# Two-layer hybrid trunk: the last norm's sums on ScalarE, residual steps behind each head's output on GpSimd, and a new order of TensorE's work in the tail

## The chip, the cores and the metric

The kernel runs on one core of a Trainium2 chip, as one launch. The metric is the device time of the launch in microseconds, the median of a few runs. The engines are TensorE (PE; its weight loads are listed apart as PEld), VectorE (DVE), ScalarE (ACT), GpSimd (POOL) and SyncE (SP), which only issues DMAs here. Each engine takes its own instructions strictly in order; between engines they wait on semaphores.

## The reference

Five blocks of 128 tokens (`TT = 5`: four latent blocks, and one context block with the index `TS = 4`), width 1024, two layers, float32. Layer 0 is gated attention. Layer 1 is a gated linear recurrence with 8 heads of 128, run in both directions. Cut to what this change touches:

```python
for i in range(DEPTH):                      # DEPTH = 2
    sh, sc, g = _adaln(cond, ada_w[i], ada_b[i])
    h = x * (1.0 + sc) + sh
    if i % 2 == 0:
        out, ... = attention(h, ...)
    else:
        out, s_fw, s_bw = _rec_mix(h, s0_fw, s0_bw, w_in, lb, norm_gain, w_out)
    x = _layer_norm(DEEPNORM_ALPHA * x + g * out, ln_gain[i], ln_bias[i])

def _rec_mix(...):                          # per head
    q, f_fw, f_bw, i_in, g = split(h @ w_in)
    o = scan forward (k_fw, v, log f_fw) + scan backward (k_bw, v, log f_bw)
    o = _rms_norm(o, norm_gain)
    return (o * silu(g)) @ w_out, s_fw, s_bw

def _layer_norm(x, g, b):
    mu  = mean(x);  var = mean((x - mu) ** 2)
    return (x - mu) * rsqrt(var + LN_EPS) * g + b
```

## The kernel before

Products of float32 matrices are made as three matmuls of split operands: a rounded part (`hi`, a cast on ScalarE, line 223) and the rest (`lo`, a subtraction on VectorE, line 224). `split_piece` makes both from a weight piece that SyncE has loaded.

**Layer 1, the loop over heads.** `proj_gen(h)` makes head h's projections: long runs of matmuls into `vgps` and `rps`, evacuated to `A` (keys and queries of both directions), `T` (decays), `v` and `g`. `gla_gen(h)` is the recurrence, in steps that end in a `yield`: seven *levels* (`lev` 0 to 6, blocks of 1 to 64 tokens: 20 small matmuls into `lv`, then on VectorE the keys, line 1276, the decays, line 1280, and the queries, line 1281, scaled for the next level; up to level 3 a copy `kc` on ScalarE; after level 4 a further block `dg`, and four copies into `At` on GpSimd, line 1295), then the *key turn* (`kp`, transposes), the *states* (`sp`), the output (`op`: squares on ScalarE, `rsqrt` into `rstdo`, two VectorE instructions, lines 1343 and 1345), and the last turn (`oT`, then `ghi` on ScalarE and `glo` on VectorE). The steps of head h are laid between the projections of head h + 1 by the class `Lane`, which counts the TensorE time that the main generator yields and compares it with due times (`D_GLA`, `D_LEV`, `D_KT`, `D_ST`, `D_OUT`). So TensorE has projection matmuls between two levels. A scheduler then orders each engine's instructions by what is ready and by where the code emitted them; what is pinned with `keep_in_program_order` stays as written.

`rsqrt` is a scale-and-add on VectorE (line 191, `rs_t`) and a power on GpSimd (line 192).

**Residual steps.** The class `Residual` prepares what the last norm adds: for each of 4 column pieces and 5 token blocks it loads 128x256 of layer 0's output (`rx<-x1d`), multiplies by `ln_g` (line 1379), adds `ln_b` (line 1380) and stores it (`x1a<-rx`), all on GpSimd's queue, all pinned. One `residual.step()` finishes the pieces that the step before loaded, and loads up to two more. `gla_gen` calls it twice a head: at the end of level 4, after the copies into `At`, and in the output step behind `rsqrt`. Thirteen steps do all 20 pieces.

**The tail.** After the last projections only head 7's recurrence is left. Now `weave` lays one step of `tail_gen` behind each step of that recurrence. A step has products of the output projection of layer 1 (`out_part(tt, ks)`: token block tt, heads ks, six matmuls of 512 columns for each head), splits of `w_out` (`wo_split(n)`), and *spreads*: `spread(1, i, ...)` makes a quarter of the gate rows `gate[1]`, 128 rows from a column by four matmuls with an identity (`gateps`, eight passes in the profile), and a copy of the bank to SBUF on VectorE (line 308). PSUM holds four tiles of two banks: token blocks 0 and 1 (later 2) keep one each, and everything else takes turns in the rest. Then `Norm(1, tt)` finishes the five blocks in order: blocks 0 to 2 lack head 7 alone, blocks 3 and 4 are whole. `part` multiplies by the gate (line 1026), adds the residual (line 1027) and takes `bn_stats` (line 1028); `finish` takes the aggregate (line 1033), `rsqrt`, and scales (lines 1042 and 1043, in two halves of 512 columns), and stores one half from SyncE and one from ScalarE. Block 4 comes in four parts of 256 columns.

Of the kernel before, what the change touches and what calls it, by code (L numbers as in the profile page):

```python
# [11 lines left out]
F32 = mybir.dt.float32  # L12
F32R = mybir.dt.float32r
U8 = mybir.dt.uint8
AF = mybir.ActivationFunctionType
ALU = mybir.AluOpType
AX = mybir.AxisListType

P = 128
D = 1024  # L20
KT = D // P
TS = 4
TT = 5
NT = TT * P
CW = 256
# [7 lines left out]
LN_EPS = 1e-5  # L33
# [99 lines left out]
def hybrid_step(ctx: ExitStack, tc: tile.TileContext, a: dict, o: dict):  # L133
    nc = tc.nc
# [53 lines left out]
    def rsqrt(out, in_, scale, eps):  # L188
        n = in_.shape[-1]
        t = tiny.tile([P, NKV * TT], F32, tag="rs", name="rs_t")  # L190
        nc.vector.tensor_scalar(t[:, :n], in_, scale, eps, ALU.mult, ALU.add)  # L191
        nc.gpsimd.tensor_tensor(out, t[:, :n], mhalf[:, :n], ALU.pow)
# [105 lines left out]
        nc.vector.tensor_tensor(gcol, src, bias, ALU.add)  # L298
        return None if layer else lambda: spread(layer, c4, gcol)

    def spread(layer, c4, gcol):

        ps = bank1("gateps")
        for s in range(2):
            for j in range(2):
                col = bass.AP(gcol.tensor, gcol.offset + 2 * j + s, [list(gcol.ap[0]), [0, P]])
                nc.tensor.matmul(ps[:, (2 * s + j) * P:(2 * s + j + 1) * P], col, ident, start=True, stop=True)
        nc.vector.tensor_copy(gate[layer][:, :, c4 * CW:(c4 + 1) * CW], ps[:].rearrange("p (a b) -> p a b", a=2))

    def ada_gen(chunks):  # L310
        todo, last = None, None
# [73 lines left out]
    gate = [None, None]  # L385
# [622 lines left out]
    class Norm:  # L1008
        def __init__(self, layer, tt, ps=None, parts=2):
            self.layer, self.tt, self.w = layer, tt, D // parts  # L1010
            if layer == 0:
                ps = bank2("outp")
            self.ps = ps and [ps[:, nh, :] for nh in range(2)]
            if layer == 0:
                self.x = lnp.tile([P, D], F32, tag="x", name="x", bufs=2)
                nc.scalar.dma_start(self.x, xd[tt])
            else:
                self.x = resid.pop(tt)
            self.y = lnp.tile([P, D], F32, tag="y", name="y", bufs=2)
            self.st = tiny.tile([P, parts, 6], F32, tag=f"st{parts}", name="st")  # L1020

        def part(self, n, ps):
            s = slice(n * self.w, (n + 1) * self.w)
            y = self.y[:, s]
            g = gate[self.layer][:, 1 if self.tt == TS else 0, s]
            nc.vector.tensor_tensor(y, ps, g, ALU.mult)  # L1026
            nc.vector.scalar_tensor_tensor(y, self.x[:, s], ALPHA, y, ALU.mult, ALU.add)  # L1027
            nc.vector.bn_stats(self.st[:, n, :], y)  # L1028

        def finish(self):  # L1030
            x, y = self.x, self.y
            mv = tiny.tile([P, 2], F32, tag="mv", name="mv")
            nc.vector.bn_aggr(mv, self.st[:].rearrange("p a b -> p (a b)"))  # L1033
            rt = tiny.tile([P, 8], F32, tag="rstd", name="rstdl")
            rstd = rt[:, 0:1]
            rsqrt(rstd, mv[:, 1:2], 1.0, LN_EPS)
            for nh in range(2):
                s = slice(nh * 512, (nh + 1) * 512)
                if self.layer == 0:
                    nc.vector.tensor_scalar(y[:, s], y[:, s], mv[:, 0:1], rstd, ALU.subtract, ALU.mult)  # L1040
                else:
                    nc.vector.scalar_tensor_tensor(x[:, s], y[:, s], mv[:, 0:1], lng[:, s], ALU.subtract, ALU.mult)  # L1042
                    nc.vector.scalar_tensor_tensor(x[:, s], x[:, s], rstd, lnb[:, s], ALU.mult, ALU.add)  # L1043
                    (nc.sync, nc.scalar)[nh].dma_start(yd[self.tt][:, s], x[:, s])
            if self.layer == 0:
                nc.sync.dma_start(x1d[self.tt], y)

    drain(split_gs(range(6, 8)))
    h1hi = gsp.tile([P, KT, NT], F32R, tag="gs", name="h1hi")
# [178 lines left out]
    def gla_gen(h, H, last=False):  # L1228
# [30 lines left out]
        for lev in range(7):  # L1259
            nb = NT // (2 * w)  # L1260
            pt = wide(bank2("lv"))
            for c in range(TT):
                if lev < 5:
                    for b in range(4):
                        t0 = c * P + 32 * b
                        queue(nc.tensor.matmul(pt[32 * b:32 * b + 32, 32 * c:32 * c + 32], kc[:, t0:t0 + 32],  # L1266
                                               view(A, QB + t0, [[2 * w, 16 // w], [QF - QB + w, 2], [1, w]]),
                                               start=True, stop=True), c + b == 0)
                else:
                    for b in range(P // w):  # L1270
                        ko, qo = (KB, QB) if b % 2 else (KF, QF)
                        s0, t0 = c * P + w * b, c * P + w * (b ^ 1)
                        queue(nc.tensor.matmul(pt[w * b:w * b + w, w * c:w * c + w], A[:, ko + s0:ko + s0 + w],
                                               A[:, qo + t0:qo + t0 + w], start=True, stop=True), c + b == 0)
            kv = view(A, KF, [[KB - KF + w, 2], [2 * w, nb], [1, w]])
            nc.vector.tensor_tensor(kv, kv, view(cur, 1, [[2 * nb - 1, 2], [2, nb], [0, w]]), ALU.mult)
            if lev < 4:
                kc = kcopy(2 * w)
            qv = view(A, QB, [[QF - QB + w, 2], [2 * w, nb], [1, w]])
            nc.vector.tensor_tensor(view(nxt, 0, [[1, 2 * nb]]), view(cur, 0, [[2, 2 * nb]]), view(cur, 1, [[2, 2 * nb]]), ALU.mult)  # L1280
            nc.vector.tensor_tensor(qv, qv, view(cur, 2 * nb + 1, [[-2 * nb - 1, 2], [2, nb], [0, w]]), ALU.mult)
            if lev == 0:
                nc.scalar.copy(near, pt[:, :32 * TT])
            elif lev < 5:
                merge(lev, pt)
            if lev == 4:
                pt = wide(bank2("dg"))
                for c in range(TT):
                    for b in range(4):
                        t = slice(c * P + b * 32, c * P + (b + 1) * 32)  # L1290
                        nc.tensor.matmul(pt[32 * b:32 * b + 32, 32 * c:32 * c + 32], H["kd"][:, t], H["q"][:, t], start=True, stop=True)
                merge(0, pt)
                for b in range(4):
                    r = slice(32 * b, 32 * b + 32)
                    nc.gpsimd.tensor_copy(blocks(At[r, :], P)[:, :, r], blocks(near[r, :], 32))  # L1295
                residual.step()
            elif lev > 4:
                for b in range(P // w):
                    r, o_ = slice(w * b, w * b + w), slice(w * (b ^ 1), w * (b ^ 1) + w)
                    nc.scalar.copy(blocks(At[r, :], P)[:, :, o_], blocks(pt[r, :w * TT], w))  # L1300
            cur, nxt = nxt, cur
            w *= 2
            yield D_LEV
# [35 lines left out]
            nc.scalar.activation(on[:, cc], opw[:, cc], AF.Square, accum_out=ss[:, c:c + 1])  # L1339
        rstd = tiny.tile([P, 8], F32, tag="rstd", name="rstdo")  # L1340
        rsqrt(rstd[:, :TT], ss[:, :TT], 1.0 / P, NORM_EPS)
        residual.step()
        nc.vector.tensor_tensor(on[:].rearrange("p (a b) -> p a b", a=TT), opw[:, :NT].rearrange("p (a b) -> p a b", a=TT),
                                view(rstd, 0, [[1, TT], [0, P]]), ALU.mult)
# [68 lines left out]
    def out_part(tt, ks):  # L1413
        if tt not in outs:
            outs[tt] = bank2("outp")
        for k in ks:
            for nh in range(2):
                out_mms(outs[tt][:, nh, :], tt, nh, ghi, glo, [k], queued=(k, nh) == (ks[0], 0))

    for h in range(RH):  # L1420
        H = {} if h else H
        for n, dt in enumerate(proj_gen(h, H, False) if h else first):
            lane.advance(dt)
            if h == RH - 1 and n in (12, 14, 20, 21):
                wo_split((12, 14, 20, 21).index(n))
        if h == RH - 1:
            out_part(0, (0, 1))
        lane.add(gla_gen(h, H, h == RH - 1))
    while residual.todo or residual.live:
        residual.step()  # L1430
# [4 lines left out]

    def tail_gen():
        yield
        out_part(1, (0, 1))
        lane.finish(1)
        wo_split(4)  # L1440
        yield
        splits = iter((5, 6, 7))
        for tt, ks in ((0, (2, 3)), (1, (2, 3)), (0, (4, 5)), (1, (4, 5)), (0, (6,)), (1, (6,))):
            out_part(tt, ks)
            for n in splits:
                wo_split(n)
                break
            yield
        gate[1] = g2.tile([P, 2, D], F32, tag="A", name="gate1")
        for i in range(4):  # L1450
            spread(1, i, gcol1[:, i])
            if i % 2:
                yield
        out_part(2, (0, 1, 2))
        yield
        out_part(2, (3, 4, 5, 6))
        yield

    resid = {}
# [115 lines left out]
```

## Time and profile before

| | |
|---|---|
| time, median of 3 runs | 878.02 us (876.84 to 880.31) |
| the profiled execution | 877.56 us, its span 875.8 us, mean granted TensorE clock 0.992 |
| TensorE busy | 828.6 us (95%) |
| VectorE busy | 533.2 us (61%) |
| ScalarE busy | 369.9 us (42%) |
| GpSimd busy | 205.5 us (23%) |
| loop over heads of layer 1 | about 440 to 788 us of the span |
| tail | about 788 us to the end |

How to read the rows: a row of the timeline has the start in us, the duration in us, the engine, the line of the kernel, the instruction, output <- inputs, sizes, the count, and in brackets how long its engine stood idle before it and for whom. A row of the chain has start, duration, engine, output and line. A row of waits has engine, output and line <- whom it waited for, then us in total, times, and the longest. A row of windows has the stretch, its length, and busy us with the count of instructions of PE, PEld, DVE, ACT and POOL, then granted clock, DMA share and GB/s. A row of groups has line, engine, instruction and count | busy us, mean ns | idle time before. A row of DMA issues ends with count, KB each, and us from issue to landing. "Busy" of TensorE is modelled, since matmuls overlap.

### The profile page before, as it was taken

Reading aid. Unit: us, or ns where it says so; the run is one execution under the profiler, and the core shown is the slowest. Engines: PE = TensorE matmul, PEld = TensorE weight load, DVE = VectorE, ACT = ScalarE, POOL = GpSimd, SP = SyncE. Lnnn points to the kernel's source line nnn. Section 1 sums busy time; section 2 is a strip of 40 time slices with the busy share of each in tenths; the row PEclk is TensorE's granted clock in tenths of the full one; section 3 lists DMA queues with packets and bytes.
Section 4 is the critical chain, followed back from the end, with each engine's and each line's share of the span. In section 5 each row is a group of like instructions: output and inputs, shape, how many; then the busy total and the mean of one; then the engine's idle time right before and its main releaser. Section 6 shows DMA issues by size and latency. Waiting matters only on the chain. (4 is left out here: it accounts for less than half of the span.)

```text
span 875.8 us, 19258 instructions
## 1 busy us (share of the span) xinstructions
PE 828.6 (95%) x8124; PEld 736.7 (84%) x8124; DVE 533.2 (61%) x966; ACT 369.9 (42%) x732; POOL 205.5 (23%) x247
## 2 busy tenths in 40 slices
PE   6898999989999899899999999999999999999895
PEld 3588999878877666678999999999999999997785
DVE  3457335565746655586637486666667575848468
ACT  2232436544745765612434453444444434444200
POOL 0132002422424643610000132233232212111111
PEclk9999999999999999999999999999999999999998
DMA  9931112212212037171232313222322323212113
GB/s 358 407 113 55 61 61 73 98 49 98 97 49 98 1 124 261 56 280 60 72 97 65 91 55 120 61 98 79 101 83 68 81 90 109 89 47 74 55 52 117
DMA packets 30182, 89.86 MB, mean 103 GB/s; under 512 B 4400, under 2 KB 9008, under 8 KB 29072
## 3 DMA queue, kind: packets, MB, share of 16 engines
q1 hardware_dynamic: 19728, 72.03, 23.2%
q0 software_dynamic: 3168, 9.31, 4.0%
q10 hardware_dynamic: 7200, 7.29, 2.6%
q8 instruction: 64, 1.05, 0.5%
q14 instruction: 22, 0.18, 0.1%
HBM read 79.44 MB, written 9.18 MB: 101 GB/s over the span
## 5 line engine op out<-in xcount | busy, mean ns | idle before, releaser
L1128 PE MATMUL rps<-h1hi,rhi 128*128 128x320 f32 x368 | 117.0, 318 | 0.0
L1129 PE MATMUL rps<-h1lo,rhi 128*128 128x320 f32 x368 | 113.5, 308 | 0.0
L1130 PE MATMUL rps<-h1hi,rlo 128*128 128x320 f32 x368 | 113.4, 308 | 0.0
L832 POOL TENSOR_SCALAR p<-p,rc 128x640 f32<-128x640 f32 x64 | 54.1, 847 | 95.2 <-DVE rc L831 84.0
L224 DVE TENSOR_TENSOR rlo<-raw,rhi 128x1024 fp32r<-128x1024 f32 x32 | 46.1, 1444 | 42.7 <-ACT rhi L223 42.7
L1128 PEld LDWEIGHTS rps<-h1hi,rhi 128*128 128x128 f32 x368 | 69.2, 188 | 1.3
L1130 PEld LDWEIGHTS rps<-h1hi,rlo 128*128 128x128 f32 x368 | 69.1, 188 | 0.2 <-DVE rlo L224 0.2
L1129 PEld LDWEIGHTS rps<-h1lo,rhi 128*128 128x128 f32 x368 | 69.0, 188 | 0.0
L824 DVE TENSOR_REDUCE nm<-sc 128x1 f32<-128x640 f32 x64 | 52.3, 820 | 25.0 <-PE sc L731 24.5
L827 ACT ACTIVATE p<-sc,nm 128x640 f32<-128x640 f32 x64 | 51.1, 799 | 25.7 <-DVE nm L824 18.6
L223 ACT CAST rhi<-raw 128x1024 fp32r<-128x1024 f32 x32 | 33.5, 1050 | 60.4 <-PE rps L1129 56.2
L839 PE MATMUL pt<-ident,p 128*128 128x128 f32 x320 | 50.7, 278 | 5.3 <-POOL p L832 3.1
L1239 ACT COPY kc<-A 128x640 f32<-128x640 f32 x40 | 32.5, 812 | 51.0 <-PE lv L1266 31.8
L1118 PE MATMUL vgps<-rhi,h1hi 128*128 128x256 f32 x180 | 51.1, 284 | 0.0
L1120 PE MATMUL vgps<-rhi,h1lo 128*128 128x256 f32 x180 | 50.7, 282 | 0.0
L1119 PE MATMUL vgps<-rlo,h1hi 128*128 128x256 f32 x180 | 50.4, 280 | 0.0
L735 ACT COPY pts<-pt 128x512 f32<-128x512 f32 x64 | 36.2, 589 | 31.6 <-PE pt L839 31.3
L1295 POOL COPY At<-near 32x160 f32<-32x160 f32 x32 | 10.0, 313 | 165.6 <-DVE near L1256 164.6
L839 PEld LDWEIGHTS pt<-ident,p 128*128 128x128 f32 x320 | 37.3, 142 | 13.5 <-POOL p L832 4.8
L730 PE MATMUL sc<-kk,X 128*128 128x320 f32 x128 | 43.5, 347 | 2.4 <-ACT p L827 2.2
L335 PE MATMUL gps<-hhi,whi 128*128 128x320 f32 x128 | 40.8, 319 | 2.4 <-ACT X L589 2.4
L1118 PE MATMUL vgps<-wspare,h1hi 128*128 128x256 f32 x140 | 41.6, 297 | 0.0
(265 smaller groups left out, 2403.2 us busy)
## 6 DMA issues: line engine op xcount, KB each, us to landing
raw<-in_rec_w_in SPq DMA_DIRECT2D x40, 512.0 KB, 4.3
raw<-in_ada_w SPq DMA_DIRECT2D x32, 512.0 KB, 3.9
raw<-in_ada_w SPq DMA_DIRECT2D x8, 1024.0 KB, 11.2
raw<-in_attn_w_in SPq DMA_DIRECT2D x16, 512.0 KB, 5.0
raw<-in_attn_w_out SPq DMA_DIRECT2D x8, 512.0 KB, 5.4
raw<-in_rec_w_out SPq DMA_DIRECT2D x8, 512.0 KB, 4.2
h<-in_xT SPq DMA_DIRECT2D x8, 320.0 KB, 10.0
x1d<-y SPq DMA_DIRECT2D x5, 512.0 KB, 2.8
```

The costliest lines, as they stand in the source:

```text
L224: pin((lo_eng or nc.gpsimd).tensor_tensor(lo, raw, hi.bitcast(F32), ALU.subtract))
L730: nc.tensor.matmul(out, X[:, h, t0:t0 + P], kk[:, c, k0:k1], start=True, stop=False)
L824: nc.vector.tensor_reduce(nm[:, 0:1], sc[:, :, :320], AX.XY, ALU.max, negate=True)
L827: nc.scalar.activation(halves(p[:]), sc[:, :, :320], AF.Exp, bias=nm[:, 0:1], accum_out=su[:, 0:1])
L832: nc.gpsimd.tensor_scalar(p, p, rs[:, 0:1], 1.0, ALU.mult, ALU.mult)
L839: nc.tensor.transpose(pt[:, i * 256 + q * P:i * 256 + (q + 1) * P], ps[q][:, (k0 + i) * P:(k0 + i + 1) * P], ident)
L1118: nc.tensor.matmul(out, h1hi[:, k, t], hi, start=(k == 0), stop=False)
L1119: nc.tensor.matmul(out, h1hi[:, k, t], lo, start=False, stop=False)
L1120: nc.tensor.matmul(out, h1lo[:, k, t], hi, start=False, stop=(k == KT - 1))
L1128: nc.tensor.matmul(ps[:, j, :320], hi[:, k, :], h1hi[:, k, t], start=(k == 0), stop=False)
L1129: nc.tensor.matmul(ps[:, j, :320], hi[:, k, :], h1lo[:, k, t], start=False, stop=False)
L1130: nc.tensor.matmul(ps[:, j, :320], lo[:, k, :], h1hi[:, k, t], start=False, stop=(k == KT - 1))
```

## The change

Three edits, and a fourth that serves the third:

- `Norm` of layer 1, token blocks 0 to 3: no `bn_stats`. `finish_two_pass` sums `y` on ScalarE (a copy into a scrap tile with an accumulated sum), makes minus the mean there, and sums the squares of the centred values in a second pass. VectorE's two scalings are 1024 columns wide, and the store is one DMA on SyncE. Block 4 keeps its form.
- `gla_gen`: the residual step at the end of level 4 goes; the output step calls two.
- `tail_gen`: products and spreads are dealt out anew. One head of block 1 moves ahead of head 7's level 0; the levels have fewer products; the four spreads lie at levels 2 to 5; 12 products each lie behind the key turn and the states, 24 behind the output, 6 behind the last turn.
- The copy of a spread of layer 1 runs on ScalarE.

```diff
-    def spread(layer, c4, gcol):
+    def spread(layer, c4, gcol, eng=None):
...
-        nc.vector.tensor_copy(gate[layer][:, :, c4 * CW:(c4 + 1) * CW], ps[:].rearrange("p (a b) -> p a b", a=2))
+        (eng or nc.vector.tensor_copy)(gate[layer][:, :, c4 * CW:(c4 + 1) * CW], ps[:].rearrange("p (a b) -> p a b", a=2))
...
+            self.two_pass = layer == 1 and tt < TS
...
-            nc.vector.bn_stats(self.st[:, n, :], y)
+            if not self.two_pass:
+                nc.vector.bn_stats(self.st[:, n, :], y)
...
+            if self.two_pass:
+                return self.finish_two_pass(rstd)
...
+        def finish_two_pass(self, rstd):
+            x, y = self.x, self.y
+            junk = lnp.tile([P, D], F32, tag="sq", name="sq")
+            sums = tiny.tile([P, 4], F32, tag="mv2", name="mv2")
+            nc.scalar.activation(junk, y, AF.Copy, accum_out=sums[:, 0:1])
+            nc.scalar.mul(sums[:, 1:2], sums[:, 0:1], -1.0 / D)
+            nc.scalar.activation(junk, y, AF.Square, bias=sums[:, 1:2], accum_out=sums[:, 2:3])
+            nc.vector.scalar_tensor_tensor(x, y, sums[:, 1:2], lng, ALU.add, ALU.mult)
+            rsqrt(rstd, sums[:, 2:3], 1.0 / D, LN_EPS)
+            nc.vector.scalar_tensor_tensor(x, x, rstd, lnb, ALU.mult, ALU.add)
+            nc.sync.dma_start(yd[self.tt], x)
...
                     nc.gpsimd.tensor_copy(blocks(At[r, :], P)[:, :, r], blocks(near[r, :], 32))
-                residual.step()
...
         rsqrt(rstd[:, :TT], ss[:, :TT], 1.0 / P, NORM_EPS)
         residual.step()
+        residual.step()
...
         if h == RH - 1:
             out_part(0, (0, 1))
+            out_part(1, (0,))
...
     def tail_gen():
         yield
-        out_part(1, (0, 1))
+        out_part(1, (1,))
         lane.finish(1)
+        out_part(0, (2,))
         wo_split(4)
         yield
-        splits = iter((5, 6, 7))
-        for tt, ks in ((0, (2, 3)), (1, (2, 3)), (0, (4, 5)), (1, (4, 5)), (0, (6,)), (1, (6,))):
-            out_part(tt, ks)
-            for n in splits:
-                wo_split(n)
-                break
+        out_part(0, (3,))
+        out_part(1, (2,))
+        wo_split(5)
+        yield
+        gate[1] = g2.tile([P, 2, D], F32, tag="A", name="gate1")
+        for i, (tt, k) in enumerate(((1, 3), (0, 4), (0, 5), (1, 4))):
+            out_part(tt, (k,))
+            spread(1, i, gcol1[:, i], nc.scalar.copy)
+            if i < 2:
+                wo_split(6 + i)
             yield
-        gate[1] = g2.tile([P, 2, D], F32, tag="A", name="gate1")
-        for i in range(4):
-            spread(1, i, gcol1[:, i])
-            if i % 2:
-                yield
-        out_part(2, (0, 1, 2))
+        out_part(1, (5,))
         yield
-        out_part(2, (3, 4, 5, 6))
+        out_part(0, (6,))
+        out_part(1, (6,))
+        yield
+        out_part(2, (0, 1))
+        yield
+        out_part(2, (2, 3, 4, 5))
+        yield
+        out_part(2, (6,))
         yield
```

GpSimd in the loop over heads, before, from the copies into `At` of head 1 to its power (`rstdo`) and on; each `rx` product pair with its store is one residual piece:

```order
L1295 COPY At<-near 32x5x32 x4
L1379 TENSOR_TENSOR rx<-rx,ln_g 128x256
L1380 TENSOR_TENSOR rx<-rx,ln_b 128x256
L1381 DMA x1a_95<-rx 128x256
L1379 TENSOR_TENSOR rx<-rx,ln_g 128x256
L1380 TENSOR_TENSOR rx<-rx,ln_b 128x256
L1381 DMA x1a_96<-rx 128x256
L1373 DMA rx<-x1d_92 128x256
L192 TENSOR_TENSOR rstdo<-rs_t,mhalf 128x5
L1379 TENSOR_TENSOR rx<-rx,ln_g 128x256
L1380 TENSOR_TENSOR rx<-rx,ln_b 128x256
L1381 DMA x1a_97<-rx 128x256
```

The same place now (line numbers are 16 higher):

```order
L1311 COPY At<-near 32x5x32 x4
L192 TENSOR_TENSOR rstdo<-rs_t,mhalf 128x5
L1395 TENSOR_TENSOR rx<-rx,ln_g 128x256
L1396 TENSOR_TENSOR rx<-rx,ln_b 128x256
L1397 DMA x1a_95<-rx 128x256
L1395 TENSOR_TENSOR rx<-rx,ln_g 128x256
L1396 TENSOR_TENSOR rx<-rx,ln_b 128x256
L1397 DMA x1a_96<-rx 128x256
L1389 DMA rx<-x1d_92 128x256
L1395 TENSOR_TENSOR rx<-rx,ln_g 128x256
L1396 TENSOR_TENSOR rx<-rx,ln_b 128x256
L1397 DMA x1a_97<-rx 128x256
```

The pieces keep their order; the power has moved ahead of all of them.

TensorE in the tail, before, from head 7's key turn (`kp`) over the states (`sp`) to the output (`op`):

```order
L1307 MATMUL kp<-ident,A 128x128 x8
L307 MATMUL gateps<-ident,gcol_82 128x128 x8
L1313 MATMUL sp<-v,kt 128x128 x8
L307 MATMUL gateps<-ident,gcol_82 128x128 x8
L1331 MATMUL op<-v,At 128x128
```

And now, around level 4 (`lv`, then `dg`), with a spread (`gateps`) on each side and half the products (`outp`) that stood there:

```order
L307 MATMUL gateps<-ident,gcol_82 128x128 x4
L1282 MATMUL lv<-A,kc 32x32 x20
L1307 MATMUL dg<-q,kd 32x32 x20
L1002 MATMUL outp<-w_9421,ghi 128x512
L1005 MATMUL outp<-w_9421,ghi 128x512
L1006 MATMUL outp<-w_9421,glo 128x512
L1002 MATMUL outp<-w_9421,ghi 128x512
L1005 MATMUL outp<-w_9421,ghi 128x512
L1006 MATMUL outp<-w_9421,glo 128x512
L307 MATMUL gateps<-ident,gcol_82 128x128 x4
L1289 MATMUL lv<-A 32x32 x20
```

The spreads have left the key turn and the states, where 12 `outp` rows each stand now, and lie between levels.

VectorE in the last norms, before, from block 0's `bn_stats` to block 1's sum (`y` is double buffered; `x` with a number is one block's residual and result):

```order
L1028 BN_STATS st<-y 128x6 x2
L1026 TENSOR_TENSOR y<-outp,gate_9672 128x512
L1033 BN_AGGR mv<-st 128x2
L1026 TENSOR_TENSOR y<-outp,gate_9672 128x512
L191 TENSOR_SCALAR rs_t<-mv 128x1
L1042 SCALAR_TENSOR_TENSOR x_9353<-y,mv,ln_9799 128x512 x2
L1043 SCALAR_TENSOR_TENSOR x_9353<-x_9353,rstdl,ln_9799 128x512 x2
L1027 SCALAR_TENSOR_TENSOR y<-x_9355,y 128x512 x2
```

And now, from block 0's sum to block 2's first gate product:

```order
L1028 SCALAR_TENSOR_TENSOR y<-x_9360,y 128x512 x2
L1027 TENSOR_TENSOR y<-outp,gate_9493 128x512 x2
L1028 SCALAR_TENSOR_TENSOR y<-x_9362,y 128x512
L1059 SCALAR_TENSOR_TENSOR x_9360<-y,mv_9816,ln_9799 128x1024
L191 TENSOR_SCALAR rs_t<-mv_9816 128x1
L1028 SCALAR_TENSOR_TENSOR y<-x_9362,y 128x512
L1061 SCALAR_TENSOR_TENSOR x_9360<-x_9360,rstdl,ln_9799 128x1024
L1027 TENSOR_TENSOR y<-outp,gate_9493 128x512
```

Between the sum of block 0 and its first scaling stand three instructions of block 1, and between `rs_t` and the second scaling one sum.

More of the change, by code (lines that the diff above doesn't have):

```diff
@@ L1027, in part @@
             nc.vector.scalar_tensor_tensor(y, self.x[:, s], ALPHA, y, ALU.mult, ALU.add)
-            nc.vector.bn_stats(self.st[:, n, :], y)
+            if not self.two_pass:
+                nc.vector.bn_stats(self.st[:, n, :], y)
         def finish(self):
             x, y = self.x, self.y
+            rt = tiny.tile([P, 8], F32, tag="rstd", name="rstdl")
+            rstd = rt[:, 0:1]
+            if self.two_pass:
+                return self.finish_two_pass(rstd)
             mv = tiny.tile([P, 2], F32, tag="mv", name="mv")
             nc.vector.bn_aggr(mv, self.st[:].rearrange("p a b -> p (a b)"))
-            rt = tiny.tile([P, 8], F32, tag="rstd", name="rstdl")
-            rstd = rt[:, 0:1]
             rsqrt(rstd, mv[:, 1:2], 1.0, LN_EPS)
```

## The prediction

> **What bounds the kernel now.** I read the busy table first, then TensorE's waits in the loop over heads, then the instructions in order of time around those waits, and last the chain that ended last.
>
> ```profile
> span 875.8 us, 19258 instructions
> PE 828.6 (95%) x8124; PEld 736.7 (84%) x8124; DVE 533.2 (61%) x966; ACT 369.9 (42%) x732; POOL 205.5 (23%) x247
> ...
> 490.00:540.00 50.00, 49.18 (x640) 47.64 (x639) 32.31 (x49) 21.28 (x43) 13.71 (x20) 1.00 0.27 83
> ...
> 590.00:640.00 50.00, 50.00 (x646) 48.51 (x645) 34.11 (x57) 23.51 (x47) 12.25 (x19) 1.00 0.30 85
> ...
> PE lv L1273 <- DVE A L1281: 3.2, 4, 0.8
> ```
>
> TensorE is the bound: in the loop it works 50.00 us of a 50 us stretch, or 49.18 where it waits once. The last row is nearly all it waits for there: four times 0.8 us, at the `lv` matmuls of the last two levels, for VectorE's line 1281. VectorE itself is busy 32 of 50 us, so this is a late instruction, not a full engine. One of the four follows, GpSimd, VectorE and TensorE in turn; the first VectorE row is the same line 1281 in the head before, where no product stood beside it:
>
> ```profile
> 531.07 0.74 POOL L1380 TENSOR_TENSOR rx<-rx,ln_b 128x256 f32<-128x256 f32 x1
> 532.72 0.75 POOL L1379 TENSOR_TENSOR rx<-rx,ln_g 128x256 f32<-128x256 f32 x1
> 533.55 1.20 POOL L1380 TENSOR_TENSOR rx<-rx,ln_b 128x256 f32<-128x256 f32 x1
> ...
> 485.61 0.82 DVE L1281 TENSOR_TENSOR A<-A,Tb 128x640 f32<-128x640 f32 x1
> ...
> 532.41 1.75 DVE L1281 TENSOR_TENSOR A<-A,Tb 128x640 f32<-128x640 f32 x1
> ...
> 534.31 0.80 PE L1273 MATMUL lv<-A 128*64 128x64 f32 x20 [0.82 <-DVE A L1281]
> ```
>
> Line 1281 takes 0.82 us alone and 1.75 beside the residual step's products on GpSimd, and TensorE stands for 0.82 us. So the price of a step at level 4 is this wait, in each of the four heads whose step has two pieces.
>
> The tail (head 7's recurrence, from about 790 us) has TensorE waits of its own, and the end belongs to VectorE:
>
> ```profile
> 792.80 0.62 PE L1266 MATMUL lv<-A,kc 128*32 128x32 f32 x40 [0.59 <-ACT kc L1239]
> 813.42 0.80 PE L1273 MATMUL lv<-A 128*64 128x64 f32 x20 [0.15 <-DVE A L1281]
> 817.80 1.16 PE L307 MATMUL gateps<-ident,gcol 128*128 128x128 f32 x8 [0.21 <-ACT kt L1309]
> 823.02 1.16 PE L307 MATMUL gateps<-ident,gcol 128*128 128x128 f32 x8 [1.38 <-DVE gate L308]
> 832.10 0.74 PE L1350 MATMUL oT<-ident,on 128*128 128x128 f32 x5 [0.90 <-DVE on L1345]
> 864.83 0.28 PE L1006 MATMUL outp<-w,glo 128*128 128x256 f32 x1
> ...
> 843.00:853.00 10.00, 10.00 (x45) 8.13 (x44) 10.00 (x20) 0.00 (x0) 3.08 (x4) 1.00 0.33 105
> ...
> 847.45 1.20 DVE y L1027 x2
> 848.65 1.20 DVE st L1028 x2
> 849.86 0.59 DVE y L1026
> ...
> 850.56 0.55 DVE y L1026
> 851.12 0.06 DVE rs_t L191
> ...
> 852.41 1.41 DVE x L1043 x2
> ...
> 869.36 0.02 issue
> ...
> 871.08 0.75 DVE x L1043
> ```
>
> The bracketed waits add up to 3.2 us. In the window row both engines work 10.00 of 10 us, and a product of 512 columns takes TensorE 10/45 = 0.22 us. The rows below it are the chain: one output tile costs VectorE 852.41 + 1.41 - 847.45 = 6.4 us, and it is never free. TensorE's last product ends at 865.1, VectorE at 871.08 + 0.75 = 871.8, 6.7 us later.
>
> **The change, part by part.**
>
> *Residual steps behind `rstdo`.* Nothing is removed: the same 20 pieces, each with a load, two products and a store, all on GpSimd's queue. At level 4 the products go away from lines 1276 and 1281, which takes away 4 x 0.8 = 3.2 us. They now stand behind the power of the head's output, as the second of two steps. What is there now:
>
> ```profile
> 506.04 1.31 DVE L1345 TENSOR_TENSOR on<-on,g 128x640 f32<-128x640 f32 x1
> 508.13 0.71 PE L1350 MATMUL oT<-ident,on 128*128 128x128 f32 x5
> 513.86 0.55 POOL L1373 DMA_DIRECT2D rx<-x1d  x1 [2.37 <-DMA x1a<-rx]
> 514.19 0.82 DVE L1281 TENSOR_TENSOR A<-A,T 128x640 f32<-128x640 f32 x1
> 516.63 0.56 PE L1266 MATMUL lv<-A,kc 128*32 128x32 f32 x40
> 517.23 0.83 DVE L1281 TENSOR_TENSOR A<-A,Tb 128x640 f32<-128x640 f32 x1 [0.75 <-PE lv L1266]
> 520.16 0.56 PE L1266 MATMUL lv<-A,kc 128*32 128x32 f32 x40
> ...
> rx<-x1d POOLq DMA_DIRECT2D x20, 128.0 KB, 3.9
> ```
>
> The first step is as before there, and TensorE's `oT` did not wait in spite of the stretched line 1345. The second step waits on GpSimd's own queue for the first one's stores and loads; its last load is issued at 513.9 and lands 3.9 later, near 518. So its four products fall between about 514 and 520, in levels 0 to 2. There line 1281 is done at 515.0 and its matmul starts at 516.6 (1.6 us spare), then 518.1 against 520.2 (2.1 spare). At level 5 the stretch was 0.93 us. Bounds for the new wait: 0 where spare time holds, 0.8 a head if the old wait comes back. I take 0, since 0.93 is nearer to nothing than to 1.6. Queued behind the waiting GpSimd instruction is only the next head's copies into `At`, at level 4, after 10 us and more. Term: -3.2 us, bounds -3.2 and 0.
>
> The trace's rows 1.75 against 0.82 are what the Trainium skill's page "SBUF — State Buffer", section "Who interferes with whom", states: a VectorE instruction with two SBUF inputs contends with a GpSimd instruction that reads SBUF. That page of the Trainium skill makes it a full block by whoever issued first. This row shows 0.93 us lost beside products of 0.75 and 1.20, so the trace agrees that they contend; what the full block would do in the new place is the third rival.
>
> *Tail: products between head 7's steps.* The count of matmuls is the same, so what counts is which waits they fill. Six products (1.3 us) more stand ahead of level 0: the 0.59 goes. Twelve (2.7 us) stand behind the key turn and twelve behind the states, in place of the spreads: 0.21 and 1.38 go. 24 in place of 18 stand ahead of `oT`: 1.3 us more against 0.90. With the 0.15 of level 6, which a spread now covers, that is all of the 3.2 us. Against this, the four spreads now stand at levels 2 to 5, on banks that must be free: the gate's copy goes from VectorE to ScalarE, among the `kc` copies and casts, and a split (1.22 us, the first row of the next part) now stands on VectorE between the two merges of level 4:
>
> ```profile
> 809.58 0.34 DVE L1256 COPY_PREDICATED near<-masks,dg 128x160 f32<-128x160 uint8 x1
> 811.11 0.56 PE L1273 MATMUL lv<-A 128*32 128x32 f32 x40
> ```
>
> The second merge ended at 809.9, 1.2 us before level 5's matmuls, whose bank it frees. With the split ahead of it, and with 6 products and a spread (1.3 + 1.2) as fill where 12 products (2.7) stood, it is about 0.2 late. The `dg` block, which now waits for a gate copy, I put at 0.3, and at 0.5 the three more places where TensorE goes from output products to another kind of matmul (estimates: between the bounds nothing and the 0.59 of the first row above). New waits: 1.0 us, bounds 0 and 3.2. Term: -2.2 us, bounds -3.2 and 0.
>
> *The last norm on ScalarE.* For tiles 0 to 3 VectorE loses `bn_stats` (1.20) and the small aggregate. Its two pairs of 512 columns become two instructions of 1024, for which this is the row, with ScalarE's and GpSimd's prices:
>
> ```profile
> L224 DVE TENSOR_TENSOR w<-raw,w 128x1024 fp32r<-128x1024 f32 x4 | 4.9, 1216 | 0.0
> L223 ACT CAST w<-raw 128x1024 fp32r<-128x1024 f32 x4 | 4.2, 1044 | 0.0
> L1339 ACT ACTIVATION_READ_ACCUMULATOR on<-op 128x1 f32 x10 | 2.1, 211 | 0.0
> L192 POOL TENSOR_TENSOR rstdl<-rs_t,mhalf 128x1 f32<-128x1 f32 x5 | 4.8, 965 | 34.7 <-DVE rs_t L191 34.7
> ```
>
> ScalarE needs 1.04 + 0.21 for the sum, about 0.21 for the small product and 1.04 + 0.21 for the squares, 2.7 us a tile, and was idle here. VectorE comes to the mean's reader 1.7 us after `y` (two gate products and one sum of the next tile) when the mean, after 1.5, is there, and to `rs_t` after 2.9 against 2.7: it just fits. Then the power takes 1.0 us on GpSimd, 1.1 with its signals, and VectorE's order puts only one sum in it (0.60 for tiles 0 and 1, 0.33 for 2 and 3): new waits of 0.5, 0.5, 0.8, 0.8. A tile costs 0.59 + 0.55 + 1.20 + 0.06 + 2 x 1.22 + 0.65 = 5.5 us instead of 6.4, 3.6 us less in four. But the end cannot come closer to TensorE's last product than the last tile's own chain, which keeps its form: three instructions of 256 columns (half of 0.59 each, 0.9) and 871.8 - 869.4 = 2.5, with 0.1 for the signal 3.5 us instead of 6.7. So at most 3.2 of the 3.6 count; 0.4 less for waits on ScalarE that so narrow a fit hides badly. Term: -2.8, bounds -3.2 and, if each tile waits as long as it gains, 0. The stores stay hidden: the last tile's two halves are issued as before.
>
> **Sum.** -3.2 - 2.2 - 2.8 = -8.2 us. The profiled execution took 877.56 us (its span 875.8 and 1.8 around it), 0.46 below the median of 878.02. So 867.6 of span, 869.4 for such a run, 869.8 against the median, 0.9% faster. Half a per cent, 4.4 us, is about what a measurement of this kernel can tell from no change: faster means below 873.6.
>
> **Rivals.**
>
> *The old wait comes back.* If a stretched line 1281, at whatever level, still stops TensorE in four heads, the 3.2 us stay: 873.0. For it: the same two engines run the same instructions. Against it: 1.6 us of spare time.
>
> *The tail's waits only move.* The level chain is too short for spreads: gate copies and casts queue on ScalarE ahead of `kc`, TensorE loses the whole 3.2 again and the second term is 0: 872.0. For it: VectorE's and ScalarE's queues are tight at levels 1 to 4. Against: the fill between two levels, 2.5 us, is hardly shorter than the 2.7 before.
>
> *Contention moves to levels 0 to 2 and grows (slower).* If VectorE stands still for all four products of a second step, it loses 0.75 + 0.74 + 0.75 + 1.20 = 3.4 us (the three products shown, the fourth as long as the first two) in one level with 1.6 to spare: 1.8 us in each of the four heads with two pieces there, +7.2 in place of -3.2, 880.2. It ends slower than before from 1.25 us a head, where four heads eat the other 5.0. For it: loads that land together put the products close. Against: the stretch shown was 0.93 for three products. By the full block of the Trainium skill's page "SBUF — State Buffer" this case is what one would expect, and the trace bears it out by half.
>
> *ScalarE is late.* If a pass with a sum takes more than the cast's 1.04 by d, each tile waits 2d - 0.25 more. From d = 0.55, 4 x 0.85 = 3.4 us, the last term is gone: 872.6. Nothing in the trace shows a 1024-wide pass with a sum.
>
> **How the numbers follow.** Forecast 0.72; old wait back 0.10; tail's waits move 0.09; contention grows 0.04; ScalarE late 0.05. The range: all three terms at their better bounds give 868.4, and 2 us more for stretched instructions elsewhere that TensorE feels below the list gives 866.2; above, 874.0 takes in each single loss (872.0, 872.6, 873.0) and 1 us. What is left out is contention and two losses together. Faster by more than 0.5%: the forecast, and most of the single losses, 0.87. Within 0.5%: 0.10. Slower by more: 0.03, half of the contention case with its price doubled.
>
> **What would show it.** Right: no wait of the last levels' `lv` for line 1281's successor, and line 1281 stretched only in levels 0 to 2; the 1.38 and 0.90 gone from the tail; VectorE's tile period near 5.5 and its end about 4 us behind TensorE's last product. Wrong: TensorE waits at levels 1 to 5 of the tail above 1.5 us in all; VectorE waiting for ScalarE's sums; `lv` waiting at level 1 or 2 in the loop.

## The result, and the profile after

| | before | changed |
|---|---|---|
| median of 4 runs | 878.09 us (876.84 to 880.31) | 868.81 us (868.16 to 869.45) |
| ratio | | 0.9892, 95% interval 0.9874 to 0.9911 |
| profiled execution | 877.56 us, span 875.8 | 869.45 us, span 867.7 |

The kernel became 9.3 us faster, 1.1%; the forecast was 869.8 us and 0.9%. The busy rows and windows of the page and of the trace, as shown of before:

```profile
span 867.7 us, 19265 instructions
PE 828.9 (96%) x8124; PEld 738.4 (85%) x8124; DVE 527.3 (61%) x942; ACT 383.1 (44%) x756; POOL 208.1 (24%) x247
...
490.00:540.00 50.00, 50.00 (x644) 48.47 (x643) 31.36 (x52) 21.02 (x42) 11.04 (x17) 1.00 0.31 91
```

TensorE does the same work; it waits less. The window that held 49.18 us of work holds 50.00, and VectorE is hardly freer than it was: 527 us in place of 533.

Where did the time come from? The first level of the recurrence begins at another moment in each execution, and not in order of what was changed: its first `lv` row starts at 466.31 us before and at 467.66 in the changed kernel, between 465.6 and 467.8 in the runs below, among them kernels whose program up to there is the same. So the traces are compared from that row on. The rows: first level, states of head 6, TensorE's last product, VectorE's last instruction, of before (whose last product is shown above):

```profile
466.31 0.63 PE L1266 MATMUL lv<-A,kc 128*32 128x32 f32 x40
...
777.45 1.95 PE L1313 MATMUL sp<-v,kt 128*128 128x128 f32 x16
...
871.08 1.41 DVE L1043 SCALAR_TENSOR_TENSOR x<-x,rstdl,ln 128x512 f32<-128x512 f32 x2
```

and of the changed kernel:

```profile
467.66 0.62 PE L1282 MATMUL lv<-A,kc 128*32 128x32 f32 x40
...
776.10 1.95 PE L1328 MATMUL sp<-v,kt 128*128 128x128 f32 x16
...
859.84 0.28 PE L1006 MATMUL outp<-w,glo 128*128 128x256 f32 x1
...
863.22 1.41 DVE L1047 SCALAR_TENSOR_TENSOR x<-x,rstdl,ln 128x512 f32<-128x512 f32 x2
```

| stretch | before | changed | difference | forecast |
|---|---|---|---|---|
| first level to states of head 6 (loop) | 311.14 | 308.44 | -2.70 | -3.2 |
| states of head 6 to TensorE's end (tail) | 87.66 | 84.02 | -3.64 | -2.2 |
| TensorE's end to VectorE's end (last norm) | 7.38 | 4.51 | -2.87 | -2.8 |
| VectorE's end to the end of the span | 3.31 | 3.07 | -0.24 | 0 |
| sum | 409.49 | 400.04 | -9.45 | -8.2 |

The two profiled spans differ by only 8.1 us, because the changed one began its loop 1.35 us later. So it is luck that the changed span, 867.7 us, lies so close to the 867.6 of the forecast: the stretches gained 9.45 us, not 8.2. The granted clock reads 1.00 in both traces from the first level to TensorE's last product, so the clock has no part in the first two differences.

*Loop.* GpSimd, VectorE and TensorE in the first head's new place (line numbers are 16 higher):

```profile
516.11 0.75 POOL L1395 TENSOR_TENSOR rx<-rx,ln_g 128x256 f32<-128x256 f32 x1
516.93 1.21 POOL L1396 TENSOR_TENSOR rx<-rx,ln_b 128x256 f32<-128x256 f32 x1
...
516.12 1.43 DVE L1292 TENSOR_TENSOR A<-A,Tb 128x640 f32<-128x640 f32 x1
517.47 1.02 DVE L1296 TENSOR_TENSOR T<-Tb 128x320 f32<-128x320 f32 x1
518.08 0.56 PE L1282 MATMUL lv<-A,kc 128*32 128x32 f32 x40
518.68 0.83 DVE L1297 TENSOR_TENSOR A<-A,Tb 128x640 f32<-128x640 f32 x1 [0.19 <-PE lv L1282]
```

The products run from 513 to 518 (forecast: about 514 to 520), and the contention now stretches lines 1292 (1.43 us) and 1296 (1.02). Line 1297, the old 1281, is short again in this head, and the next `lv` has no wait in brackets. In the last head with two pieces there, four instructions in a row are stretched, line 1297 among them:

```profile
749.72 1.37 DVE L1297 TENSOR_TENSOR A<-A,T 128x640 f32<-128x640 f32 x1
751.00 1.35 DVE L1292 TENSOR_TENSOR A<-A,Tb 128x640 f32<-128x640 f32 x1
752.28 1.41 DVE L1296 TENSOR_TENSOR T<-Tb 128x320 f32<-128x320 f32 x1
753.61 1.36 DVE L1297 TENSOR_TENSOR A<-A,Tb 128x640 f32<-128x640 f32 x1
...
755.79 0.56 PE L1282 MATMUL lv<-A,kc 128*32 128x32 f32 x40
```

They take 5.5 us in place of 3.0 (0.82, 0.83, 0.48 and 0.83 elsewhere), so VectorE loses 2.5 us in two levels; it is done at 754.97, 0.8 us before the next `lv`. From the first level to the states of head 6 TensorE's list of waits is empty.

*Tail.* The last product ahead of level 0, before and now, then the rows of the changed kernel that answer to those with 0.59, 0.21, 1.38 and 0.90 us of waiting, and the one new wait:

```profile
791.83 0.39 PE L1006 MATMUL outp<-whi,glo 128*128 128x512 f32 x1
...
791.91 0.39 PE L1006 MATMUL outp<-whi,glo 128*128 128x512 f32 x1
792.23 0.62 PE L1282 MATMUL lv<-A,kc 128*32 128x32 f32 x40
806.49 0.56 PE L1307 MATMUL dg<-q,kd 128*32 128x32 f32 x40 [0.18 <-ACT gate L308]
808.56 0.33 DVE L1272 COPY_PREDICATED near<-masks,dg 128x160 f32<-128x160 uint8 x1
809.47 0.56 PE L1289 MATMUL lv<-A 128*32 128x32 f32 x40
...
815.45 0.48 PE L1002 MATMUL outp<-w,ghi 128*128 128x512 f32 x1
820.04 0.48 PE L1002 MATMUL outp<-w,ghi 128*128 128x512 f32 x1
831.31 0.71 PE L1366 MATMUL oT<-ident,on 128*128 128x128 f32 x5
```

There is no bracket but 0.18. From the start of the last product to the start of level 0 it took 792.80 - 791.83 = 0.97 us before and takes 0.32 now: that wait cost 0.65 us, a little more than its bracket. The second merge of level 4, behind the split now, ends at 808.89, 0.6 us before the matmuls that need its bank: the spread ahead of them covers it.

*Last norm.* ScalarE's passes for block 0, VectorE's readers, and VectorE's waits in the whole stage:

```profile
837.75 1.06 ACT L1056 ACTIVATE sq<-y 128x1024 f32<-128x1024 f32 x1 [4.89 <-DVE y L1028]
838.71 0.18 ACT L1056 ACTIVATION_READ_ACCUMULATOR sq<-y 128x1 f32 x1
838.93 0.20 ACT L1057 ACTIVATE mv<-mv 128x1 f32<-128x1 f32 x1
839.16 1.16 ACT L1058 ACTIVATE sq<-y,mv 128x1024 f32<-128x1024 f32 x1
839.30 1.28 DVE L1059 SCALAR_TENSOR_TENSOR x<-y,mv,ln 128x1024 f32<-128x1024 f32 x1
840.49 0.15 DVE L191 TENSOR_SCALAR rs_t<-mv 128x1 f32<-128x1 f32 x1
...
DVE x L1061 <- POOL rstdl L192: 1.6, 4, 0.5
...
860.15 0.42 DVE L1027 TENSOR_TENSOR y<-outp,gate 128x256 f32<-128x256 f32 x1
...
861.53 0.26 DVE L1039 BATCH_NORM_AGGREGATE mv<-st 128x2 f32<-128x24 f32 x1
```

VectorE never waits for ScalarE's sums. It waits for the power in each of the four blocks, 1.6 us together. The last two rows are block 4: VectorE takes up TensorE's last product, which ends at 860.12, at 860.15, so its queue no longer sets the end; only the last block's own chain stands behind TensorE.

### The profile page after: what moved, and what is told of

It is laid out like the page before. It is cut to its first block, busy times and chain, and to the rows that moved or that the text cites. A ratio compares the mean times of both kernels' runs of the same rounds, so it can differ in the third digit from the quotient of the medians.

```text
span 867.7 us, 19265 instructions
## 1 busy us (share of the span) xinstructions
PE 828.9 (96%) x8124; PEld 738.4 (85%) x8124; DVE 527.3 (61%) x942; ACT 383.1 (44%) x756; POOL 208.1 (24%) x247
## 3 DMA queue, kind: packets, MB, share of 16 engines
q8 instruction: 64, 1.05, 0.5%
## 4 chain that ended last, share of the span: by engine, by line
PE 84%; DMA 5%; DVE 4%; ACT 3%; POOL 2%; issue 2%; DVEq 0%; SPq 0%; ACTq 0%; POOLq 0%
PE rps L1144 7%; PE rps L1146 7%; PE rps L1145 6%; PE vgps L1134 5%; PE outp L1002 4%; PE vgps L1136 4%; PE vgps L1135 4%; PE outp L1005 4%; PE outp L1006 4%; PE pot L757 4%; PE pt L839 3%; PE lv L1282 2%; PE adaps L264 2%; PE sc L730 2%; PE gps L335 2%; PE gps L337 2%
## 5 line engine op out<-in xcount | busy, mean ns | idle before, releaser
L224 DVE TENSOR_TENSOR rlo<-raw,rhi 128x1024 fp32r<-128x1024 f32 x32 | 44.1, 1380 | 46.1 <-ACT rhi L223 46.1
L192 POOL TENSOR_TENSOR rstdo<-rs_t,mhalf 128x5 f32<-128x5 f32 x8 | 9.5, 1192 | 162.4 <-DVE rs_t L191 162.4
```

## The experiments

Each ran beside the kernel before on the same chip; the ratio is to that kernel. Lengths in a trace are from the first `lv` row, as above.

### The residual steps alone

```diff
@@ gla_gen, level 4
-                residual.step()
@@ gla_gen, output
         residual.step()
+        residual.step()
```

> The kernel before with one edit: both residual steps behind the power of each head's output, none at level 4. Theory (stretched line 1281 was the only price of the step at level 4): the four waits of 0.8 us go and about 0.1 us a head comes back, as head periods of 46.84 us in the changed kernel against 46.73 and 47.58 before show: 2.0 to 3.2 us faster, ratio about 0.9970. Rival (the contention only moves): within 0.5 us of before, with TensorE waits at levels 0 to 2. In the trace: no wait of the level-5 and level-6 matmuls for VectorE.

874.02 us, ratio 0.9962 (0.9949 to 0.9975). From the first level to the states of head 6 it takes 775.03 - 467.42 = 307.61 us, 3.53 less than before:

```profile
467.42 0.63 PE L1266 MATMUL lv<-A,kc 128*32 128x32 f32 x40
...
588.19 1.95 PE L1312 MATMUL sp<-v,kt 128*128 128x128 f32 x16
634.91 1.95 PE L1312 MATMUL sp<-v,kt 128*128 128x128 f32 x16
...
775.03 1.95 PE L1312 MATMUL sp<-v,kt 128*128 128x128 f32 x16
```

That is more than the four waits of 0.8 and a little more than expected, and the gain is not handed back: a head takes 634.91 - 588.19 = 46.72 us here, where the changed kernel takes 46.84. The theory stands; its 0.1 us a head does not belong to this edit.

### The new tail alone

The new `tail_gen`, the product moved ahead of level 0, and the spreads' copies on ScalarE; residual steps and norm as before.

> The kernel before with the new tail alone (products, spreads, and the spreads' copies on ScalarE); residual steps and last norm as before. Theory: TensorE's waits in the tail go, 3.2 to 3.7 us, and since VectorE is busy without a gap from its first gate product to the end, that whole block starts and ends as much earlier: 3.2 to 3.7 us faster, ratio about 0.996, VectorE's lag behind TensorE's last product 7.4 us as before. Rival (VectorE's five norms are the bound and swallow it): under 1 us faster and a lag of 10 us or more.

873.30 us, ratio 0.9959 (0.9945 to 0.9974), 3.6 us. States of head 6 to TensorE's end: 83.9 us, as in the changed kernel; the only wait of TensorE in the tail is 0.2 us of `dg` for a gate copy. VectorE's lag stays at 868.2 - 860.6 = 7.6 us. The whole block of norms moved, nothing was swallowed.

### The new norm alone

> The kernel before with the new last norm alone (sums of blocks 0 to 3 on ScalarE). Theory: TensorE ends where it did, VectorE's lag behind its last product falls from 7.4 us to about 4.4, 3.0 us faster, ratio about 0.9966. Rival (VectorE waits for ScalarE and GpSimd as long as it saves): within 0.5 us of before. Rival (the two edits of the tail help each other): less than 2 us here and less than 3 in the run with the new tail alone, though both together give 6.6.

875.10 us, ratio 0.9972 (0.9963 to 0.9980), 2.5 us. VectorE's lag is 870.6 - 866.1 = 4.5 us in place of 7.4, as forecast. The three ratios of the parts add up to 0.38 + 0.41 + 0.28 = 1.07%, and all three together gave 1.08%: within the intervals they neither hide nor help each other. In the traces, from the first level to the end of the span, the parts gain 3.51, 3.54 and 2.36 us, together 9.41 against 9.45. But here a head without a wait took 46.84 us, and no edit of this kernel touches the loop.

### The spreads' copies back on VectorE

```diff
-            spread(1, i, gcol1[:, i], nc.scalar.copy)
+            spread(1, i, gcol1[:, i])
```

> The changed kernel, but the four spreads' copies back on VectorE. Theory (VectorE was full at levels 1 to 4: scalings, splits and merges): four copies of 0.69 us among them delay line 1281's successor and the merges, and TensorE waits 1 to 2 us in the tail: 1 to 2 us slower than the changed kernel. Rival (the copies' engine does not matter, levels have spare time): within 0.4 us of the changed kernel.

869.33 us, ratio 0.9906 (0.9891 to 0.9921), against 868.81 (and 868.68 in the repeat below): the times can't tell the two apart. The trace tells more, because this execution began its loop early (466.07): from there the span is 401.5 us long, 1.5 more than the 400.0 of the changed kernel. Of this 1.3 lie in the tail (85.3 us from the states of head 6 to TensorE's end, in place of 84.0), where TensorE waits:

```profile
PE gateps L307 <- DVE T L1296: 0.9, 1, 0.9
PE lv L1282 <- DVE near L1272: 0.2, 1, 0.2
```

So the engine of the copies is worth about 1.3 us in one trace, as the theory has it, and no time confirms it. The rest of the tail's gain, 2.4 of 3.6 us, comes from where the products and spreads stand; which place gives how much was not tried apart.

### Fills in place of the products at level 4

The kernel before, with this in the step at level 4 only; the loads and stores stay, and the residual of those pieces is left out.

```diff
-                pin(nc.gpsimd.tensor_tensor(t, t, self.gb[0], ALU.mult))
-                pin(nc.gpsimd.tensor_tensor(t, t, self.gb[1], ALU.add))
+                for _ in range(2):
+                    pin(nc.gpsimd.memset(t, 0.0))
+                    pin(nc.gpsimd.memset(t, 0.0))
```

> The kernel before, the residual step left at level 4, but there its two products a piece are left out and four fills of the same tile stand in their place (the residual of those pieces is not computed; loads and stores stay). Theory (VectorE's line 1281 with two SBUF inputs is slowed by GpSimd's reads of SBUF): fills read nothing, line 1281 takes 0.82 us at level 5 again, TensorE's four waits of 0.8 us are gone, about 3 us faster than before, like the run with the residual steps alone. Rival (any GpSimd instruction or store there slows VectorE): line 1281 stays near 1.75 us and the four waits stay. If the fills are much shorter than the products, a remaining stretch of 0.1 to 0.4 us would leave it open.

874.58 us, ratio 0.9954 (0.9937 to 0.9971), and 307.6 us from the first level to the states of head 6, like the residual steps alone. GpSimd and VectorE in the place that was shown of before:

```profile
532.55 0.31 POOL L1382 MEMSET rx<- 128x256 f32 x1
533.16 0.55 POOL L1386 DMA_DIRECT2D x1a<-rx  x1 [0.30 <-POOL rx L1382]
533.70 0.33 POOL L1381 MEMSET rx<- 128x256 f32 x1
534.09 0.31 POOL L1382 MEMSET rx<- 128x256 f32 x1
...
532.77 0.82 DVE L1276 TENSOR_TENSOR A<-A,Tb 128x640 f32<-128x640 f32 x1 [2.92 <-PE lv L1273]
...
533.52 0.82 DVE L1281 TENSOR_TENSOR A<-A,Tb 128x640 f32<-128x640 f32 x1
```

GpSimd is at work beside line 1281, with stores too, and the line takes 0.82 us. So neither GpSimd's being busy nor its writing stretches the line. What the fills lack is the products' reading of SBUF, which is therefore the likely cause; the fills are also shorter (0.31 us in place of 0.75), but no part of the stretch is left. With this run the trace also agrees with the second half of the rule in the Trainium skill's page "SBUF — State Buffer", "Who interferes with whom": a VectorE instruction with two SBUF inputs does not contend with a GpSimd instruction that only writes.

### Every residual product three times

```diff
-                pin(nc.gpsimd.tensor_tensor(t, t, self.gb[0], ALU.mult))
-                pin(nc.gpsimd.tensor_tensor(t, t, self.gb[1], ALU.add))
+                for _ in range(3):
+                    pin(nc.gpsimd.tensor_tensor(t, t, self.gb[0], ALU.mult))
+                    pin(nc.gpsimd.tensor_tensor(t, t, self.gb[1], ALU.add))
```

> The changed kernel with every residual product made three times in its place behind the head's output (the residual is then another number). Theory (1.6 and 2.1 us of spare time at levels 0 and 1, about 1 us at each later level): 12 products of about 0.8 us in place of 4 run through levels 0 to 4; VectorE loses up to 3 x 1.5 us over them; some waits of TensorE come back, 0 to 1 us a head, 0 to 6 us slower than the changed kernel. Rival (the new place has room without limit): no TensorE wait in the loop and within 0.5 us. Rival (the new place was at its limit): more than 8 us slower.

883.20 us, ratio 1.0054 (1.0035 to 1.0073): 14.4 us slower than the changed kernel, and slower than before. The theory's 0 to 6 us was wrong; what came is the rival in which the new place was at its limit (more than 8 us).

```profile
PE lv L1282 <- DVE A L1297: 11.7, 9, 2.0
PE lv L1289 <- DVE A L1297: 1.2, 2, 0.6
PEld lv L1282 <- ACT near L1299: 3.8, 4, 1.4
```

The same wait comes back, nearly always at the levels up to 4 (line 1282). The sum behind the expectation took the spare time of each level as if it could be used one after the other, and only the second step's products; the first step's, tripled too, push the second's to later levels. In one head the first step's products alone run from 554.2 to 568.6, and the second step's from 572.7 on. So one set of products fits without a wait, with 0.8 us to spare in the head shown above, and three cost 14.4 us. Two sets were not tried.

### The sums in an old tile, and the kernel before moved by 128 bytes

What made a head 46.84 us long wherever the new norm was? Its `sums` are a new tag in the pool of small tiles, 128 bytes a partition with its four buffers, and all tiles on that side of SBUF behind it move: `h1hi` from address 76864 to 76992 in the built program, `ghi`, `rhi` and `rlo` likewise by 128 bytes; `A` and `h1lo` lie on the other side and stay. Two kernels tell it apart. The changed kernel without the tag:

```diff
-                return self.finish_two_pass(rstd)
+                return self.finish_two_pass(rstd, rt[:, 4:8])
...
-            sums = tiny.tile([P, 4], F32, tag="mv2", name="mv2")
```

> The changed kernel, but the three sums of the last norm lie in unused columns of the tile that holds its rstd, so the pool of small tiles has no new tag and every tile behind it keeps the address of the kernel before (the new tag moves them by 128 bytes). Theory (the 0.12 us a head that came back in every run with the new norm is the moved addresses): head periods of 46.72 us instead of 46.84, about 1 us faster than the changed kernel. Rival (it comes from the norm's code or from chance): 46.84 as before and no difference.

and the kernel before with one:

```diff
+    pad = tiny.tile([P, 4], F32, tag="mv2", name="mv2")
+    nc.vector.memset(pad, 0.0)
```

> The kernel before with an unused small tile (128 bytes a partition with its four buffers, filled once at the start), which moves the tiles behind it by 128 bytes as the changed kernel's new tag does. Theory (addresses): head periods of 46.84 where no wait is and 47.68 where one is, as in the run with the norm alone, about 1 us slower than before. Rival (the norm's code or chance): 46.72 and 47.58, no difference.

Neighbouring states of the recurrence, one head apart, in the first of these kernels:

```profile
540.82 1.95 PE L1327 MATMUL sp<-v,kt 128*128 128x128 f32 x16
587.54 1.95 PE L1327 MATMUL sp<-v,kt 128*128 128x128 f32 x16
```

and in the second, where the last head shown has no wait:

```profile
730.52 1.95 PE L1315 MATMUL sp<-v,kt 128*128 128x128 f32 x16
777.36 1.95 PE L1315 MATMUL sp<-v,kt 128*128 128x128 f32 x16
```

A head takes 46.72 us without the tag and 46.84 with it, with the new norm or the old: the moved addresses make it, not the norm's code. The time of the second kernel can't show it (878.42 us, ratio 1.0005, 0.9995 to 1.0015); in its trace the loop is 777.36 - 465.64 = 311.72 us long, 0.6 more than before. The first took 867.21 us, ratio 0.9868 (0.9848 to 0.9888). Two of its heads took 46.9: in each, 0.2 us is lost in one step among the `rps` matmuls behind level 5, where the trace names no wait.

### Both once more on one chip

> The changed kernel once more, on one chip with the version with the sums in an old tile. Ratio to before 0.988 to 0.991, head periods of 46.84 us.

> The version with the sums in unused columns of an old tile once more, beside the changed kernel. Theory (addresses): head periods of 46.72 to 46.9 us against 46.84, 0.3 to 1.0 us faster than the changed kernel. Rival (no effect that a time can show): medians within 0.3 us, or the other way round.

868.68 us (0.9906, 0.9891 to 0.9920) and 866.86 us (0.9890, 0.9873 to 0.9906). From the first level to the end of the span the changed kernel takes 400.1 us (400.0 in the first trace) and the version without the tag 399.1 (399.6), so 0.4 to 1.0 us are in the traces; the rest of the 1.6 and 1.8 us between the medians lies ahead of the loop or is chance. The gain in time is more than the 0.3 to 1.0 us expected. With the lower time on both occasions, the version without the tag is the best one here, though the intervals overlap.

## Why the prediction was right, by its steps

- *What bounds.* This was right: TensorE's waits, and the end by VectorE. The three terms are independent, as the three runs of the parts show.
- *Residual steps, -3.2.* The mechanism is shown: without the products at level 4 the waits are gone (the steps alone), and with fills in their place too. The size was 3.5, since a wait with a bracket of 0.8 made a head 0.87 us longer (47.6 us in place of 46.72). In the changed kernel 2.7 was left; the 0.8 between them is the address effect, which no step of the prediction had. That the new place has no wait was read rightly, but the margin was not: the prediction set a loss of 0.93 us against 1.6 of spare time, while one head lost 2.5 us over two levels and had 0.8 left. The tripled products show the same.
- *Tail, -2.2.* This is the term that was mis-sized: 3.6 us were measured, outside its own bound of -3.2. All five old waits are gone, as forecast, but of the new waits of 1.0 us only 0.18 came: the bank of level 5 was free 0.6 us early (forecast: 0.2 late), `dg` waited 0.18 by the bracket (0.3), and the 0.5 for more changes of kind of matmul did not show. The old brackets also read low. Taken from start to start, against the same transition without a wait, the five waits cost 0.65, 0.23, 0.29, 1.46 and 1.05 us, 3.7 in all where the brackets add up to 3.2; so 3.2 was no bound.
- *Last norm, -2.8.* 2.9 us were measured. ScalarE's passes took 1.06 and 1.16 (1.04 was taken from a cast), VectorE's wide instructions 1.28 with overlap (1.22), and the waits for the power 1.6 us (2.6). The prediction took the end of the first half of VectorE's last instruction (871.8) for its end, which is 872.49. By its own reading the lag fell from 6.7 us to 863.22 + 0.75 - 860.12 = 3.9, as forecast, but in part by luck: the 0.4 put for waits on ScalarE did not come, and the last block's three short instructions took 861.53 - 860.15 = 1.4 us in place of 0.9. Another 0.2 us were gained after VectorE's end, where the forecast had nothing; why was not tried.
- *Rivals.* The old wait did not come back, the tail's waits did not only move, ScalarE was not late. Contention did move to levels 0 to 2, and in one head it grew to 2.5 of the 3.4 us that the rival named, but over two levels and without a wait; with three times the products it makes the kernel slower than before. Nor did the first to begin always go ahead: before, line 1281 had begun at 532.41, and GpSimd's product at 532.72 still took its usual 0.75 us.

## What to carry to other kernels

Read a stall on the bounding engine back to the one instruction that came late, and ask why that one was long: here a side job on another engine stretched it, and moving the job to a place with spare time gave the whole wait back at no cost in work. Then measure how much spare time is left there. Where the same matmuls can stand in several places, count fills against waits place by place, and give the longest fill to the longest chain. Compare traces from an anchor in the loop when the start scatters more than the edit is worth, and put small new tiles where they move no others.

## What was not expected of the hardware

Moving the tiles on one side of SBUF by 128 bytes made each head of the loop 0.12 us longer (46.84 in place of 46.72 us, in every kernel with the moved addresses, in nearly all heads without a wait), with the same instructions in the same order on TensorE. The delay gathers in steps of 0.01 to 0.02 us within the runs of `rps` matmuls, and a part of it is made up again among the `vgps` matmuls. Which of the moved tiles does it was not tried, and the cause stays open.
